# Moving all stores of a rotary-embedding kernel to SyncE's queue, in smaller pieces

## The chip, the cores and the metric

The kernel runs on one core of a Trainium2 chip. Times are microseconds (us) on the device; a kernel's time is the median of its runs. The "span" in a profile is shorter by about 1.8 us (84.47 us and 82.69 in the profiled run of the kernel before).

## The reference

```python
angles = np.outer(positions * scale, freqs)          # 1024 x 32
cos, sin = np.cos(angles), np.sin(angles)
x_first, x_second = x[..., :32], x[..., 32:]         # x: 8 x 8 x 1024 x 64, float32
out = concatenate([x_first * cos - x_second * sin,
                   x_first * sin + x_second * cos], axis=-1)
```

16.78 MB come in and 16.78 MB go out, with two multiplications and an addition per number. It is a problem of moving data.

## The kernel before

The 64 heads are cut into four units of 16 heads, 4.19 MB each. In memory a unit is 128 rows (one for each partition) of 32 KB. GpSimd loads the units and turns them into 2-byte numbers on the way (a casting load). VectorE rotates each unit in two halves, ScalarE casts each half back to 4 bytes in the tile `OUT`, and a DMA stores it. The half of the first unit that is needed last comes in by two plain loads instead, from SyncE and ScalarE.

```python
pin(nc.gpsimd.dma_start(out=Xf[0][:, :NH], in_=xv[0][:, :NH]))
...
for u in range(1, NU):
    c = C2 if u == NU - 1 else 0                       # C2 = 1024 columns
    pin(nc.gpsimd.dma_start(out=Xf[u][:, : N - c], in_=xv[u][:, : N - c]))
    if c:
        pin(nc.gpsimd.dma_start(out=Xf[u][:, N - c :], in_=xv[u][:, N - c :]))
...                                                    # tables of sine and cosine
for u in range(NU):
    OUT = xout.tile([P, N], FP32, tag="O")             # three buffers
    for s in range(2):
        ...                                            # four VectorE instructions
        pin(nc.scalar.copy(out=OUT[:, ns], in_=Xf[u][:, ns]))
        if u >= NU // 2:
            pin(nc.sync.dma_start(out=ov[u][:, ns], in_=OUT[:, ns]))
    if u < NU // 2:
        c = C1 if u == 0 else 0                        # C1 = 512 columns
        if c:
            pin(nc.gpsimd.dma_start(out=ov[u][:, :c], in_=OUT[:, :c]))
        pin(nc.gpsimd.dma_start(out=ov[u][:, c:], in_=OUT[:, c:]))
```

So the first two units are stored from GpSimd, behind the loads on the same queue, and the last two in halves from SyncE.

## Time and profile before

| | before |
|---|---|
| time, median of 6 runs (range) | 84.56 us (84.37 to 84.61) |
| span of the profiled run | 82.69 us |
| GpSimd's queue (q0): moved as it lands, share of 16 DMA engines | 15.73 MB, 66.7% |
| SyncE's queue (q1) | 9.44 MB, 27.3% |
| ScalarE's queue (q10) | 1.06 MB, 3.2% |
| VectorE, ScalarE busy | 60.3 us, 40.1 us |

The prediction takes the GB/s of a stretch to count packets at their landing, and puts the first packet at 1.3 us and the end of the last at 81.1 us. The packet records of the trace show that the views count a packet at its start. On the span's clock the first packet starts at 1.74 us and the last ends at 81.45 us. Every time of a packet below is on the span's clock.

### The profile page before, as it was taken

How to read it: one execution, taken by the hardware profiler on the slowest of the kernel's cores; microseconds unless marked ns; L12 is line 12 of the kernel's file. 1: busy time of each engine (PE TensorE's matmuls, PEld its weight loads, DVE VectorE, ACT ScalarE, POOL GpSimd, SP SyncE). 2: the span in 40 equal slices, each digit the busy share in tenths (PEclk: the TensorE clock that was granted, in tenths of full speed). 3: DMA queues.
4: the chain of work that ended last, by engine and by line, in shares of the span. 5: the costliest groups of instructions: out<-in, count | busy, mean ns of one | idle time of the engine just before them, and what ended most of it. 6: DMA issues, size and time to landing. Idle time of an engine off the chain costs nothing.

```text
span 82.7 us, 184 instructions
## 1 busy us (share of the span) xinstructions
PE 6.4 (8%) x18; PEld 2.4 (3%) x18; DVE 60.3 (73%) x40; ACT 40.1 (49%) x18; POOL 5.7 (7%) x16
## 2 busy tenths in 40 slices
PE   0011798200000000000000000000000000000000
PEld 0011232000000000000000000000000000000000
DVE  0306276999999999999999999999999997000000
ACT  0602159999960691294089049309705912950000
POOL 4950000000020002000000200000000000000000
PEclk9999999995555555555555555555555555555555
DMA  3899998996998999999499889989899899999991
GB/s 55 323 323 269 297 325 186 254 254 135 246 254 182 198 254 222 222 222 222 36 456 446 357 386 476 507 357 460 380 523 404 365 428 428 460 404 436 428 428 79
DMA packets 2099, 26.22 MB, mean 317 GB/s; under 512 B 371, under 2 KB 371, under 8 KB 563
## 3 DMA queue, kind: packets, MB, share of 16 engines
q0 software_dynamic: 1088, 15.73, 66.7%
q1 hardware_dynamic: 720, 9.44, 27.3%
q10 hardware_dynamic: 290, 1.06, 3.2%
q14 instruction: 1, 0.00, 0.0%
HBM read 16.79 MB, written 16.78 MB: 406 GB/s over the span
## 4 chain that ended last, share of the span: by engine, by line
DVE 54%; ACT 14%; issue 7%; DMA 6%; PE 5%; DVEq 1%; ACTq 0%
DVE X L158 19%; DVE pr L157 19%; DVE X L162 9%; DMA freq_row<-in_freqs_dram 6%; ACT T L144 5%; DVE X L159 5%; ACT OUT L165 4%; PE ps L134 4%; ACT X L145 4%; DVEq L203 1%; PE cfreq L102 1%; ACT tab L127 1%; DVE r L118 1%; DVE y L109 1%; ACTq L71 0%
## 5 line engine op out<-in xcount | busy, mean ns | idle before, releaser
L165 ACT CAST OUT<-X 128x4096 f32<-128x4096 f16 x8 | 28.8, 3605 | 24.2 <-DVE X L162 24.2
L157 DVE TENSOR_TENSOR pr<-X,T 128x4096 f16<-128x4096 f16 x8 | 18.3, 2292 | 1.0 <-ACT T L144 0.7
L158 DVE TENSOR_TENSOR X<-X,T 128x4096 f16<-128x4096 f16 x8 | 18.3, 2292 | 0.3
L159 DVE TENSOR_TENSOR X<-X,pr 128x2048 f16<-128x2048 f16 x8 | 9.8, 1225 | 0.3
L162 DVE TENSOR_TENSOR X<-pr,X 128x2048 f16<-128x2048 f16 x8 | 9.7, 1218 | 0.0
L144 ACT CAST T<-ps 128x1024 f16<-128x1024 f32 x6 | 5.7, 1030 | 2.6 <-PE ps L134 2.6
L134 PE MATMUL ps<-tab,sel 128*128 128x512 f16 x16 | 5.8, 503 | 2.6 <-ACT tab L127 2.2
L142 DVE CAST T<-ps 128x1024 f16<-128x1024 f32 x2 | 2.4, 1224 | 2.2 <-PE ps L134 2.2
L145 ACT CAST X<-X0f 128x4096 f16<-128x4096 f32 x1 | 3.6, 3650 | 0.0
L100 DVE COPY sel<-one 128x2048 f16<-128x2048 f16 x1 | 0.7, 694 | 2.8 <-POOL one L89 2.8
L122 ACT ACTIVATE tab<-r 128x256 f16<-128x256 f32 x1 | 0.4, 416 | 4.4 <-DVE r L118 4.4
L172 POOL DMA_DIRECT2D out_dram<-OUT x2 | 1.1, 531 | 20.2 <-ACT OUT L165 20.2
L122 ACT ACT_TABLE_LOAD x1 | 1.3, 1283 | 2.1 <-issue 2.1
L134 PEld LDWEIGHTS <-sel 128*128 128x128 f16 x16 | 1.9, 122 | 6.1 <-issue 5.7
L95 POOL DMA_DIRECT2D X<-in_x_dram x3 | 2.0, 658 | 0.0
L171 POOL DMA_DIRECT2D out_dram<-OUT x1 | 0.6, 554 | 19.1 <-ACT OUT L165 19.1
L105 DVE CAST posf<-pos_i 128x8 f32<-128x8 int32 x1 | 0.2, 173 | 2.2 <-DMA pos_i<-in_positions_dram 2.2
L102 PE MATMUL cfreq<-freq_row,coef 1*128 1x32 f32 x2 | 0.6, 391 | 5.9 <-DMA freq_row<-in_freqs_dram 5.9
L109 DVE TENSOR_TENSOR y<-posf,cfreq 128x256 f32<-128x256 f32 x1 | 0.4, 420 | 0.7 <-PE cfreq L102 0.7
L85 POOL DMA_DIRECT2D X<-in_x_dram x1 | 0.7, 669 | 0.8 <-POOLq L189 0.8
L102 PEld LDWEIGHTS cfreq<-freq_row,coef 1*128 1x128 f32 x2 | 0.5, 308 | 5.9 <-issue 5.9
L97 POOL DMA_DIRECT2D X<-in_x_dram x1 | 0.6, 557 | 0.0
(12 smaller groups left out, 2.8 us busy)
## 6 DMA issues: line engine op xcount, KB each, us to landing
out_dram<-OUT SPq DMA_DIRECT2D x4, 2048.0 KB, 11.6
X<-in_x_dram POOLq DMA_DIRECT2D x2, 2048.0 KB, 24.2
out_dram<-OUT POOLq DMA_DIRECT2D x1, 4096.0 KB, 20.4
out_dram<-OUT POOLq DMA_DIRECT2D x1, 3840.0 KB, 21.1
X<-in_x_dram POOLq DMA_DIRECT2D x1, 1792.0 KB, 37.5
X0f<-in_x_dram SPq DMA_DIRECT2D x1, 1024.0 KB, 4.7
X<-in_x_dram POOLq DMA_DIRECT2D x1, 1024.0 KB, 11.5
X0f<-in_x_dram ACTq DMA_DIRECT2D x1, 1024.0 KB, 13.4
```

The source lines that it names most:

```text
L95: pin(nc.gpsimd.dma_start(out=Xf[u][:, : N - c], in_=xv[u][:, : N - c]))
L102: nc.tensor.matmul(out=cfreq, lhsT=coef, rhs=freq_row, start=True, stop=True)
L122: pin(nc.scalar.activation(out=tab[:, 0], in_=r, func=AF.Sin, bias=0.0, scale=-_TWO_PI_DN))
L134: nc.tensor.matmul(out=ps[:, i].rearrange("p t w -> p (t w)"), lhsT=sel[:, g + i].rearrange("s h q -> s (h q)"), rhs=tab.rearrange("s t k ...
L142: pin(nc.vector.tensor_copy(out=dst, in_=ps))
L144: pin(nc.scalar.copy(out=dst, in_=ps))
L145: pin(nc.scalar.copy(out=Xf[0][:, NH:], in_=X0f[:, :NH]))
L157: pin(nc.vector.tensor_tensor(out=pr, in0=Xs, in1=sin_b, op=ALU.mult))
L158: pin(nc.vector.tensor_tensor(out=Xs, in0=Xs, in1=cos_b, op=ALU.mult))
L159: pin(nc.vector.tensor_tensor(out=Xs[:, :, 0, :], in0=Xs[:, :, 0, :], in1=pr[:, :, 1, :], op=ALU.subtract))
L162: pin(nc.vector.tensor_tensor(out=Xs[:, :, 1, :], in0=pr[:, :, 0, :], in1=Xs[:, :, 1, :], op=ALU.add))
L165: pin(nc.scalar.copy(out=OUT[:, ns], in_=Xf[u][:, ns]))
```

## The change

All stores go to SyncE. The first and the last unit leave in four DMAs each, of 8 KB rows; the two between in halves, of 16 KB rows. GpSimd is left with the loads. The intent is plain from the page: the first unit's stores wait some 18 us behind loads on GpSimd's queue (issued at 24.32 us, first row at 42.21), and on a queue of their own they could start at once.

```diff
-            if u >= NU // 2:
-                pin(nc.sync.dma_start(out=ov[u][:, ns], in_=OUT[:, ns]))
-        if u < NU // 2:
-            c = C1 if u == 0 else 0
-            if c:
-                pin(nc.gpsimd.dma_start(out=ov[u][:, :c], in_=OUT[:, :c]))
-            pin(nc.gpsimd.dma_start(out=ov[u][:, c:], in_=OUT[:, c:]))
+            parts = 2 if u in (0, NU - 1) else 1
+            for i in range(parts):
+                c = slice(s * NH + i * NH // parts, s * NH + (i + 1) * NH // parts)
+                pin(nc.sync.dma_start(out=ov[u][:, c], in_=OUT[:, c]))
```

More of the change, by code (lines that the diff above doesn't have):

```diff
@@ L47 @@
     W = K8 * half
-    C1 = 512
     C2 = 1024
```

## The prediction

> **What bounds the kernel now.** I read first the sixteen DMA engines' row over the span, then the queues with their bytes, then the table by stage, the waits of SyncE's queue, and last the chain of waits. The page has them so:
>
> ```profile
> span 82.7 us, 184 instructions
> PE 6.4 (8%) x18; PEld 2.4 (3%) x18; DVE 60.3 (73%) x40; ACT 40.1 (49%) x18; POOL 5.7 (7%) x16
> ...
> DMA  3899998996998999999499889989899899999991
> ...
> q0 software_dynamic: 1088, 15.73, 66.7%
> q1 hardware_dynamic: 720, 9.44, 27.3%
> q10 hardware_dynamic: 290, 1.06, 3.2%
> ...
> HBM read 16.79 MB, written 16.78 MB: 406 GB/s over the span
> ...
> DVE 54%; ACT 14%; issue 7%; DMA 6%; PE 5%; DVEq 1%; ACTq 0%
> ```
>
> The chain names VectorE (54%), and that misleads: it follows instructions back from the last one on an engine, and the last transfers are not in it. The three queues' packets took 66.7 + 27.3 + 3.2 = 97.2% of sixteen engines' span, so the DMA engines have something in hand from the first packet to the last. Q0 is GpSimd's queue. Its 15.73 MB are counted as they land: 8.39 MB of stores plus loads written as 2-byte numbers, which is half of what they read. So a load stretch shows about half the GB/s of a store stretch at the same pace, and has to be doubled before the two are compared:
>
> ```profile
> 1.30:4.00 2.70, 0.00 (x0) 0.00 (x0) 0.69 (x1) 1.28 (x1) 2.62 (x7) 1.00 0.84 269
> 24.00:36.00 12.00, 0.00 (x0) 0.00 (x0) 11.83 (x8) 5.00 (x3) 1.08 (x2) 0.50 1.02 218
> 38.50:42.50 4.00, 0.00 (x0) 0.00 (x0) 3.93 (x4) 0.82 (x1) 0.00 (x0) 0.50 0.91 139
> 44.00:56.00 12.00, 0.00 (x0) 0.00 (x0) 11.82 (x8) 5.12 (x3) 0.53 (x1) 0.50 1.03 444
> 68.00:80.00 12.00, 0.00 (x0) 0.00 (x0) 1.83 (x2) 3.60 (x1) 0.00 (x0) 0.50 1.00 430
> 81.10:82.70 1.60, 0.00 (x0) 0.00 (x0) 0.00 (x0) 0.00 (x0) 0.00 (x0) 0.50 0.00 0
> ```
>
> The columns are stretch, length, busy time of five engines, granted clock, DMA share and GB/s. Casting loads read 2 x 218 = 436 GB/s (24 to 36 us); stores from GpSimd go at 444 (44 to 56, where packets counted at their landing flatter it a little) and from SyncE at 430 (68 to 80). All three are one ceiling, near 432 GB/s or 27.0 bytes per ns and engine. Of the 33.57 MB moved, 33.57 / 432 = 77.7 us are pure transfer. The rest of 82.7 is 1.3 us before the first packet, 1.6 us after the last (receipt and closing), and about 2 us lost inside: the slow start (269 GB/s at 1.3 to 4), and one dip, at 38.5 to 42.5, where 139 GB/s land against 218. That is 4 x (1 - 139/218) = 1.5 us at most; packets in flight at its edges count against it, and I put the true loss at 1 us. The engines are "busy" all through it, so it is a stall of packets and not an empty queue. It falls where the 7168-column load of the last unit ends and its 1024-column remainder begins.
>
> The last proof is the end:
>
> ```profile
> 66.49 7.34 SPq L167 DMA_DIRECT2D out_dram<-OUT  x2
> ...
> 69.86 3.60 ACT L165 CAST OUT<-X 128x4096 f32<-128x4096 f16 x1 [3.40 <-DVE X L162]
> ```
>
> ScalarE ends at 73.46 and the last store of 2.10 MB is issued at once. Alone it would take 2.10 / 0.430 = 4.9 us, to 78.4. The last packet ends at 81.1: a backlog of 81.1 - 73.5 - 4.9 = 2.7 us of older stores lies ahead of it. So the arithmetic could be up to 2.7 us later, and a store could be issued earlier, without moving the end. Only bytes per ns, stalls, or an empty queue move it.
>
> **What the Trainium skill says.** "DMA: Bandwidth & Descriptors", section "Issuing engines are not separate DMA queues": DMAs from any issuing engine run on the same sixteen engines and interleave, and changing the issuer saves only sequencer time. The trace agrees: 444 and 430 GB/s for the two issuers. The same page, "Where 436 GB/s comes from", puts the ceiling at 435 GB/s for sixteen ports; the 430 to 444 here are that. The same page, "Queues, rings and completion order": each engine takes turns between queues, a packet at a time. The packet records of the trace show rows as packets: 1227 ns for a 32 KB load row, 611 ns for a 16 KB and 309 ns for an 8 KB row on q1. So after the change a load and a store queue share time by row size. "SBUF — State Buffer", "Who interferes with whom", says VectorE can starve GpSimd of the port with which it writes descriptors, and that SyncE's DMAs are immune. The trace shows nothing to win there: GpSimd's three store issues took 0.53 to 0.55 us each beside a busy VectorE, behind a queue that was full anyway.
>
> **The change part by part.** The streams of VectorE, ScalarE and TensorE are the same, instruction by instruction; GpSimd loses three issues, SyncE goes from four stores to eight. SyncE's last eight transfers gain waits on a reused completion counter; each refers to one eight transfers back, which for the last unit are the first unit's stores. By the simulation below they end by 52, against issues at 66 and 73: no cost.
>
> *Packets.* First unit: before, one piece of 0.26 MB (64 packets of 159 ns) and one of 3.93 MB (128 of 1138 ns), together 155.9 us of engine time, or 9.74 us over sixteen. After, 512 rows of 309 ns: 9.89. Second: before 128 x 1213 / 16 = 9.70, after 256 x 611 / 16 = 9.78. Third: same. Fourth: before 256 x 611 / 16 = 9.78, after 9.89. Sum +0.34 us.
>
> *Turn-taking.* The start has an example: 8 KB rows of q10 beside casting loads took 322 ns, 13 more than on q1. If every row that runs beside loads pays 13 ns: the first unit's rows then, some 300 to 500, cost 0.25 to 0.4 us.
>
> *Order.* Today the first unit's store, issued at 24.3, waits behind all loads and starts near 42. Now it starts near 26 and takes turns with them. Stepping through it packet by packet with the durations above: the third unit's load ends near 32.7 (was 31.5), the fourth's near 44 and 48 (was 41 and 42). VectorE wants them at 41.7 and 55.8 and 62.8. Margins of 9, 12 and 15 us, so no compute moves. The buffer that the fourth unit's cast reuses at 62.9 is free by about 54. The queue never empties, and the last packet comes at the same place plus the sums above.
>
> *The dip.* Up to 1.0 us could come back, if it belongs to all engines passing from long to short load packets at once, which interleaving smears. Nothing in the trace says so; I give it one half: -0.5.
>
> Total: +0.34 + 0.3 - 0.5 = +0.1 us, or nothing. The finer last pieces (8 KB rows) may even out sixteen engines' ends by 0.1 to 0.2 us. I predict 84.4.
>
> **Rivals.** First, *earlier stores shorten the tail*: the intent, I suppose. For it: stores wait 20 us today. Against it: those 20 us are a full DMA row; advancing bytes in a saturated queue only delays others, by conservation. It could give at most the 2.7 us of backlog, then the last store's own time binds: 73.5 + about 0.7 to its first packet + 4.9 + 1.6 = 80.7 us of span, time 82.5. Reaching that needs 2 us of lost time to vanish; I see 1.
>
> Second, *reads and writes mixed run at another pace*. The kernel before never mixes HBM reads with stores for long, so the trace is silent. If the 24 us of mixed stretch (26 to 50) ran 3% slower, 0.7 us are lost: 85.2; if faster by as much, 83.7.
>
> Third, *late loads stop VectorE*. If turns were not by row but favoured stores strongly, the fourth unit would come late: 8.4 MB of stores are issued before 45.3, and all of them ahead of the last loads would put these at 42 + 17 (the first four half-stores, 4.9 each, less what fits anyway) = near 59. The first half of that unit would wait 3 us; with 2.7 us of backlog as cushion, 0.5 us appears at the end, plus some empty queue: up to 86. Unlikely.
>
> Fourth, *the tail goes hollow*: if SyncE's in-order issue waits on a counter, a later store starts late. Then the share falls below full in the last ten slices; up to 85.5.
>
> **Range and chances.** The known terms cancel within half a microsecond; the dip and mixed pace give about 0.7 each way. I say 84.4, 83.4 to 85.4. Two per cent is 1.7 us: below 82.8 is almost the floor worked out above, chance 0.05; above 86.2 needs the third or fourth rival, 0.03; the rest 0.92.
>
> **What would show it.** Right: DMA row full to the end; HBM rate over the span still near 406; VectorE's and ScalarE's starts unchanged, ScalarE ending at 73.5; packets on q1 about 16.78 + 1.05 MB; loads of the last unit landing near 44 and 48; no dip, or the same dip near 47. Wrong: VectorE waiting for X at the fourth unit; the mixed stretch at a total clearly off 432 GB/s when loads are doubled; a store stretch with 8 KB rows below 425; the span under 81.

## The result, and the profile after

The changed kernel takes 84.67 us (median of 6 runs, 84.52 to 84.79); the kernel before took 84.56 in the same rounds. The ratio is 1.0017, with a 95% interval from 1.0002 to 1.0031. Ratios here divide the mean time of one kernel's runs by that of the other's runs of the same rounds, so they are not quite the ratio of the medians. The change costs some 0.1 us and is "the same" by any practical measure. 84.4 was predicted, with 83.4 to 85.4 as the range.

The page of the changed kernel, in the lines that answer to those of before:

```profile
span 83.0 us, 195 instructions
...
DMA  2899996998998988999796999999999999899991
...
q1 hardware_dynamic: 1872, 17.83, 51.4%
q0 software_dynamic: 720, 7.34, 42.8%
q10 hardware_dynamic: 290, 1.06, 3.2%
HBM read 16.79 MB, written 16.78 MB: 404 GB/s over the span
...
X<-in_x_dram POOLq DMA_DIRECT2D x1, 1792.0 KB, 41.3
...
X<-in_x_dram POOLq DMA_DIRECT2D x1, 256.0 KB, 44.6
```

8.39 MB have moved from q0 to q1. The sum of the shares is 97.4% where it was 97.2%, and the DMA row is as full as it was. The last two loads, issued at 4.1 and 4.6 us, now land 41.3 and 44.6 us later where they took 37.5 and 38.3: they share the engines with stores. Nothing waited for them. VectorE and ScalarE run the same sequence without a new wait, only some 0.35 us earlier, which they gained in the first 20 us. Where the last half begins (62.47) no wait is marked, and the last cast waits for VectorE alone:

```profile
60.08 1.23 DVE L158 TENSOR_TENSOR X<-X,pr 128x2048 f16<-128x2048 f16 x1
61.22 1.22 DVE L161 TENSOR_TENSOR X<-pr,X 128x2048 f16<-128x2048 f16 x1
62.47 2.29 DVE L156 TENSOR_TENSOR pr<-X,T 128x4096 f16<-128x4096 f16 x1
...
69.52 3.60 ACT L164 CAST OUT<-X 128x4096 f32<-128x4096 f16 x1 [3.40 <-DVE X L161]
```

The last cast starts at 69.52 us (69.86 before), and still the end is later. The table by stage has the same columns as before:

```profile
1.30:4.00 2.70, 0.00 (x0) 0.00 (x0) 0.69 (x1) 1.28 (x1) 2.62 (x7) 1.00 0.85 281
24.00:36.00 12.00, 0.00 (x0) 0.00 (x0) 11.83 (x8) 5.32 (x2) 0.00 (x0) 0.50 1.02 235
...
44.00:56.00 12.00, 0.00 (x0) 0.00 (x0) 11.83 (x8) 5.12 (x3) 0.00 (x0) 0.50 1.02 400
...
68.00:80.00 12.00, 0.00 (x0) 0.00 (x0) 1.48 (x2) 3.60 (x1) 0.00 (x0) 0.50 1.00 425
```

From 24 to 36 us 235 GB/s stand where there were 218, and from 44 to 56 us 400 for 444: stores are now spread among the loads, and loads count half, so neither figure says that anything is faster or slower. Only the stretch from 68 to 80 us compares directly, stores against stores: 425 GB/s with mostly 8 KB rows, 430 with 16 KB rows. That is just at the 425 below which the prediction wanted to be called wrong; it is not a sharp sign, as two kernels below with 16 KB rows throughout show ("changed, all 16 KB" has 425, "all 16 KB, last counter" 434).

What did move is the dip. The next two lines are GB/s from 24 to 32 us in slices of 0.2 us, first of the kernel before, then of the changed one. Sixteen DMA engines work in step, so each group of three or four numbers is one row on each engine, and the distance between groups is the time of one row.

```profile
GB/s 0 328 901 82 0 0 0 328 901 82 0 0 0 328 901 82 0 0 0 328 901 82 0 0 0 328 901 82 0 0 0 246 901 164 0 0 0 72 645 430
```

```profile
GB/s 0 492 655 164 0 0 0 492 655 164 0 0 0 0 410 819 82 0 0 0 0 0 287 369 860 369 82 0 0 41 287 532 860 164 82 0 0 82 287 573
```

Before, a load row of 32 KB takes six slices, 1.2 us, every time. In the changed kernel the distance grows to seven slices and then to about nine before the first store rows appear (the 287 and 369 in front of the 860 are where they mix in). The packet records give 1227 ns as the usual row, up to 1511 ns for rows that start near 25.5 us and up to 1694 ns near 27. SyncE had issued its first store at 23.70; its first row starts at 28.46. So most of the slow rows come while a store is already issued and has not yet begun; some more follow between 30 and 33 us.

To size such stalls I count the bytes that each stretch moved, with casting loads at the 4 bytes they read, and compare with 27.1 bytes per ns and engine (433 GB/s), the pace of undisturbed stretches. "Lost" below is the difference as time, worked out from the packet records of each run:

| lost, us | 24-36 | 36-46 | 46-56 | 56-66 | 66-80 | last packet ends | closing after it |
|---|---|---|---|---|---|---|---|
| before | 0.01 | 1.05 | 0.01 | 0.02 | 0.07 | 81.45 | 1.24 |
| changed | 0.89 | 0.13 | 0.17 | 0.05 | 0.15 | 81.78 | 1.23 |

One loss of 1.05 us has become one of 0.89, and small ones are added: mixing in the middle, 8 KB rows at the end (0.15 for 0.07). The sum of the five stretches rises by 0.23 us, from 1.17 to 1.40 before rounding of the parts. The profiled run of the changed kernel (84.79) is the slowest of its six, so these 0.2 us are rather more than the typical difference.

### The profile page after: what moved, and what is told of

The parts are those of the page before. It is cut to its first block, busy times and chain, and to the rows that moved or that the text cites. A ratio compares the mean times of both kernels' runs of the same rounds, so it can differ in the third digit from the quotient of the medians. Undisturbed runs are those within 1.5% of the kernel's fastest.

```text
span 83.0 us, 195 instructions
## 1 busy us (share of the span) xinstructions
PE 6.1 (7%) x18; PEld 2.4 (3%) x18; DVE 60.3 (73%) x40; ACT 40.1 (48%) x18; POOL 4.1 (5%) x13
## 3 DMA queue, kind: packets, MB, share of 16 engines
q10 hardware_dynamic: 290, 1.06, 3.2%
## 4 chain that ended last, share of the span: by engine, by line
DVE 54%; ACT 15%; issue 7%; DMA 5%; PE 5%; DVEq 1%; ACTq 0%
DVE X L157 19%; DVE pr L156 19%; DVE X L161 9%; ACT T L143 6%; DMA freq_row<-in_freqs_dram 5%; DVE X L158 5%; ACT OUT L164 4%; ACT X L144 4%; PE ps L133 4%; DVEq L197 1%; PE cfreq L101 1%; ACT tab L126 1%; DVE r L117 1%; DVE y L108 1%; ACTq L70 0%
## 5 line engine op out<-in xcount | busy, mean ns | idle before, releaser
L126 ACT ACTIVATE tab<-ra,quarter 128x256 f16<-128x256 f32 x1 | 0.5, 508 | 0.0
## 6 DMA issues: line engine op xcount, KB each, us to landing
X<-in_x_dram POOLq DMA_DIRECT2D x1, 1792.0 KB, 41.3
X<-in_x_dram POOLq DMA_DIRECT2D x1, 256.0 KB, 44.6
```

## The experiments

Twelve kernels were run; all gave correct results. The medians of the kernel before in their rounds were 84.47, 84.47 and 84.44.

My theory after the result was that the loss of about 1 us belongs to the passing from loads to stores, whoever issues them and wherever it falls. The rival was that in the kernel before it belonged to the short load of 1024 columns, and in the changed kernel to something else, such as SyncE's queue starting or the number of rows.

**First group.** The first kernel is the kernel before with one load for the whole last unit:

```diff
-        c = C2 if u == NU - 1 else 0
+        c = 0
```

> The kernel before, with the last unit's load in one piece in place of 7168 + 1024 columns. Theory (the dip is the price of passing from loads to stores, whoever issues them): a dip of about 1 us stays between 38 and 42 us; only the short rows' own cost goes, 128 x (172 + 1076 - 1227) ns / 16 = 0.17 us, so 84.4. Rival (the dip is the short load's): the dip is gone and the time is near 83.5.

The other three are the changed kernel with 16 KB rows for the first unit, for the last, and for both:

```diff
-            parts = 2 if u in (0, NU - 1) else 1
+            parts = 2 if u == NU - 1 else 1      # first unit in halves
+            parts = 2 if u == 0 else 1           # or: last unit in halves
+            parts = 1                            # or: all in halves
```

> The changed kernel, with the first unit's stores in halves of 16 KB rows (last unit still in 8 KB rows). Theory: 256 rows of 611 ns for 512 of 309 save 0.11 us, and half as many turns of 13 ns save up to 0.2 us: 84.4. The dip of about 0.6 us when the stores arrive near 25 us stays, since it goes with the change of direction. Rival (the dip at 25 us comes of the number of rows): it halves, 84.1. Rival (8 KB rows protect the loads): loads are late, but with 10 us of margin this costs nothing.

> The changed kernel, with the last unit's stores in halves of 16 KB rows (first still in 8 KB rows). Theory: 8 KB rows went at 26.7 bytes per ns and engine over the last ten us against 26.95 for 16 KB rows, so 0.1 us is saved: 84.6. Rival (finer rows at the end even out the engines): 84.8.

> The changed kernel, with all stores in halves of 16 KB rows from SyncE. Theory: sum of the two parts, 84.3; what is left against the kernel before is then the move to SyncE itself, with the dip at 25 us in place of the one at 40 us. Rival (parts don't add up): outside 84.2 to 84.5.

| | time | ratio to before (95%) | lost 24-36 | lost 36-46 | last packet ends | closing |
|---|---|---|---|---|---|---|
| before, whole last load | 84.51 | 1.0001 (0.9988 to 1.0014) | 0.01 | 0.87 | 81.49 | 1.24 |
| changed, first unit 16 KB | 84.71 | 1.0026 (1.0010 to 1.0043) | 0.76 | 0.08 | 81.55 | 1.35 |
| changed, last unit 16 KB | 84.71 | 1.0028 (1.0014 to 1.0042) | 0.47 | 0.33 | 81.59 | 1.35 |
| changed, all 16 KB | 84.77 | 1.0036 (1.0020 to 1.0051) | 0.72 | 0.08 | 81.50 | 1.47 |

The first row kills the rival for most of the loss in the kernel before. Its stages, with the last load in one piece:

```profile
36.00:38.50 2.50, 0.00 (x0) 0.00 (x0) 2.47 (x2) 1.90 (x1) 0.00 (x0) 0.50 0.98 210
38.50:42.50 4.00, 0.00 (x0) 0.00 (x0) 3.93 (x4) 1.16 (x1) 0.00 (x0) 0.50 0.90 161
...
44.00:56.00 12.00, 0.00 (x0) 0.00 (x0) 11.83 (x8) 5.12 (x3) 0.53 (x1) 0.50 1.00 431
```

It reads 161 GB/s at 38.5 to 42.5 us where the kernel before had 139, still far under 218. By the packet records, without a short load 0.87 us are lost at the same place; up to 0.18 of the 1.05 could be the short load's, though the kernel before with one more 128-byte load (third group), the same up to 52 us, lost 0.91 there. The time did not go to 83.5, nor did the 0.17 us of the short rows come back in the end; the sixteen engines finished 0.67 us apart in that run where it had been 0.38, and the last of them counts.

The other three rows went against my expectation. 16 KB rows should have saved 0.1 to 0.4 us, and the times did not fall at all. The traces show two opposite halves. The last packet does end earlier, by 0.19 to 0.28 us (81.50 to 81.59 for 81.78). But the closing after the last packet is longer, 1.35 and 1.47 us in place of 1.23, and that I had not counted. Nor did the turns become fewer. In the changed kernel 288 rows of 8 KB took 322 ns in place of 309; with all rows of 16 KB, 286 rows took 624 ns in place of 611. The 13 ns came about once for each load row beside the stores, whatever the store's row, and cost 0.23 us over sixteen engines in both.

These rows also show how far a stall varies. Up to its last unit, "last unit 16 KB" is the changed kernel, instruction by instruction, and yet it lost 0.47 and 0.33 us where the other lost 0.89 and 0.13.

**Second group.** Is the loss a price paid once, as for a path that is cold at the first store? Then a tiny early store would take it away. It went into both kernels:

```diff
+    wz = consts.tile([P, 128], FP32)
+    pin(nc.vector.memset(wz, 0.0))
+    pin(nc.sync.dma_start(out=ov[NU - 1][:, N - 128 :], in_=wz))
```

> The kernel before, with a 64 KB store of zeros from SyncE at the start (overwritten by the last store). Theory A (the first store after loads only is a cold path, warmed once): the dip of 1 us near 40 us is gone and the time is near 83.6. Theory B (each passing from loads to stores costs it): dip as before, 84.5 to 84.6.

> The changed kernel with the same early store. A: the loss of 0.9 us between 24 and 34 us is gone, 83.8 to 83.9. B: it stays, 84.7.

And what of a store is it that stalls the loads? Two kernels, made from the one before, put other transfers in the place where the changed kernel has its first stores. One adds plain loads, the other copies within on-chip memory:

```diff
             pin(nc.scalar.copy(out=OUT[:, ns], in_=Xf[u][:, ns]))
+            if u == 0:      # loads
+                pin(nc.sync.dma_start(out=X0f[:, s * 2048 : (s + 1) * 2048], in_=xv[0][:, s * 2048 : (s + 1) * 2048]))
+            if u == 0:      # or: copies
+                pin(nc.sync.dma_start(out=X0f[:, NH + s * 2048 : NH + (s + 1) * 2048], in_=OUT[:, ns.start : ns.start + 2048]))
```

> The kernel before, plus two plain loads of 1 MB in 8 KB rows from SyncE near 24 us into a dead buffer: 2.1 MB more, 4.9 us, so 89.4. If the loss at 25 us in the changed kernel comes of SyncE's queue starting beside casting loads, load rows are stretched here too (near 0.6 us lost between 24 and 30). If it comes of stores, there is none, and the 1 us dip comes when the loads end, near 44 to 47.

> The kernel before, plus two copies of 1 MB in 8 KB rows from on-chip memory to on-chip memory from SyncE near 24 and 31 us: 4.9 us more, 89.4. If reading on-chip memory amid loads is what stalls, near 0.6 us is lost at 24 to 34 and the dip at the end of the loads is smaller; if writing to HBM is, nothing is lost there and the dip at the end of the loads is whole.

| | time | lost 24-36 | lost 36-46 | lost 46-56 | last packet ends | closing |
|---|---|---|---|---|---|---|
| before + early store | 85.56 | 0.02 | 0.68 | 0.01 | 82.63 | 1.65 |
| changed + early store | 85.66 | 0.29 | 0.39 | 0.18 | 81.93 | 1.67 |
| before + loads on SyncE | 89.42 | 0.11 | 0.26 | 0.36 | 86.03 | 1.61 |
| before + on-chip copies | 89.73 | 0.49 | 0.43 | 0.08 | 86.33 | 1.61 |

The early store did not pay. The ratios are 1.0124 (1.0094 to 1.0154) and 1.0143 (1.0130 to 1.0156), and 0.7 us are still lost after it in both kernels. That is less than the 1.06 and 1.03 without it (24 to 46 us), but other kernels without an early store also show 0.7 to 0.9, so I don't call it an effect. Theory A falls. About 0.4 us of the extra time are again closing, and 0.3 more lie outside the span (2.07 us between time and span in both, where it was 1.78). In the first of them one DMA engine also ended 1.66 us after the earliest, in a run that was the slowest of six that spread from 85.11 to 86.34; why was not followed up.

The last two tell the parts of a store apart. GB/s from 24 to 32 us, with the extra loads and then with the copies:

```profile
GB/s 0 82 614 532 492 82 0 0 123 246 737 451 410 0 0 0 246 451 451 737 82 0 0 123 123 737 492 410 82 0 0 205 287 614 532 328 0 0 0 246
```

```profile
GB/s 0 246 655 410 0 0 0 246 655 410 0 0 0 246 655 410 0 0 0 82 328 369 410 573 0 0 41 123 492 410 492 410 0 0 123 164 369 410 737 164
```

With loads on SyncE's queue the new rows simply mix in: 0.11 us are lost in twelve, and between 24 and 34 us no load row takes over 60 ns more than usual. In the seven kernels whose 8 or 16 KB store rows begin there, 20 to 51 load rows do, and with the copies 36. So a second queue that starts beside casting loads is not enough to slow them, and writing to HBM is not needed, since the copies read and write on-chip memory. *Reading* on-chip memory is what the copies and the stores share and the extra loads lack.

That this is the cause is not shown, for three reasons. Each of the two is one look, and the size varies as said above. The extra loads were issued at 20.3 us, both at once, and not at 24 and 31. And "issuer only" (third group) speaks against it in this form: there the 2 KB store rows of the first 512 columns, which read on-chip memory too, ran beside the loads from 28.0 us on without one slow load row up to 35 us (0.08 us lost from 24 to 34). Its loss, 0.71 us from 34 to 39, came around the first 30 KB rows, which were issued at 31.2 and began at 38.25. So the stall belongs to long or many rows at least, and its cause stays open.

The 0.43 us that the copies show between 36 and 46 us lie in the last rows of the 7168-column load, where all sixteen engines have one slow row (between 42 and 44 us). "Changed + early store" and "changed, last unit 16 KB" lost 0.39 and 0.33 in that stretch without any copies, so this part is not put to their account. With the extra loads the loss at the end of the loads is 0.26 + 0.36 = 0.62 us, just before GpSimd's stores begin at 46.8.

**Third group: the closing.** In the trace, SyncE's last records are a row of waits on completion counters. Transfers issued by SyncE and ScalarE use eight counters in turn, and at the end SyncE checks them in order. The kernel before makes 8 such transfers and the changed one 16, so in both the last store is on the eighth counter and everything else has been checked by then. The three kernels with 16 KB rows make 14, 14 and 12: counter six, six and four. The kernels of the second group end on the first or the second. The theory is that each counter checked after the last store's costs 0.06 us. To test it, four loads of 128 bytes bring "all 16 KB" to 16 transfers, and one such load brings the kernel before to 9:

```diff
+            if u == 1 and s == 1:
+                for i in range(4):
+                    pin(nc.sync.dma_start(out=pad[:, i * half : (i + 1) * half], in_=freqs[None, :]))
```

> All stores in 16 KB halves from SyncE (as in the third form tried), plus four loads of 128 bytes on SyncE's queue, so that the last store falls on the last of the eight completion counters that SyncE checks at the end, as in the kernel before and in the changed one. Theory C (closing time after the last packet is 1.66 us plus 0.06 us for each counter checked after the last store's): 1.66 us again, last packet near 81.1, span near 82.75, time 84.5 to 84.55. Rival (closing time varies for another reason): 84.7 to 84.8 as without the loads.

> The kernel before, plus one load of 128 bytes on SyncE's queue amid the last four stores, so that the last store falls on the first counter. Theory C: closing 2.1 us in place of 1.66, time 84.9. Rival: unchanged, 84.5.

Two more go with them. In one the issuer alone changes; it keeps the store shapes of the kernel before, with five such loads:

```diff
-            pin(nc.gpsimd.dma_start(out=ov[u][:, c:], in_=OUT[:, c:]))
+            pin(nc.sync.dma_start(out=ov[u][:, c:], in_=OUT[:, c:]))    # and the same for the first 512 columns
```

> The kernel before with its store shapes kept (512 + 7680 columns, 8192 columns, then halves), all issued by SyncE, with five loads of 128 bytes so that the last store is on the last counter. It is the issuer alone. Theory: one loss of about 0.9 us moves from 38-42 us to 24-34 us, rows of 30 and 32 KB keep 27.0 bytes per ns and engine, last packet near 81.0 and closing 1.66: 84.5, the same as before. Rival (moving to SyncE costs of itself): 84.7.

The last joins what had looked useful: all stores in 16 KB halves from SyncE, the last counter, and the whole last load.

> As the first of this group, with the last unit's load in one piece as well. Theory: short rows saved, 0.17 us: 84.35 to 84.4, a little under the kernel before. Rival (nothing at this level adds up, since the slowest of sixteen engines ends it): 84.5.

| | time | ratio to before (95%) | last packet ends | closing |
|---|---|---|---|---|
| all 16 KB, last counter | 84.49 | 1.0005 (0.9992 to 1.0017) | 81.48 | 1.24 |
| before, first counter | 85.05 | 1.0069 (1.0056 to 1.0081) | 81.53 | 1.64 |
| issuer only, last counter | 84.59 | 1.0016 (1.0002 to 1.0030) | 81.52 | 1.30 |
| all 16 KB, last counter, whole load | 84.26 | 0.9987 (0.9975 to 1.0000) | 81.25 | 1.23 |

The end of the DMA row shows how little time lies between the last packets. The GB/s from 80 to 84 us, in slices of 0.1 us, of the kernel before, then of the changed one, then of the kernel before with one 128-byte load:

```profile
GB/s 164 1147 328 0 492 492 164 983 492 0 0 0 0 0 0 0 0 0 0 0 0 0 0 0 0 0 0 0 0 0 0 0 0 0 0 0 0 0 0 0
```

```profile
GB/s 573 328 410 492 410 410 492 410 410 410 492 246 492 164 82 0 0 0 0 0 0 0 0 0 0 0 0 0 0 0 0 0 0 0 0 0 0 0 0 0
```

```profile
GB/s 819 492 0 492 328 492 819 328 164 164 0 0 0 0 0 0 0 0 0 0 0 0 0 0 0 0 0 0 0 0 0 0 0 0 0 0 0 0 0 0
```

A packet stands in the slice where it starts, so 0.61 us have to be added for a 16 KB row and 0.31 for an 8 KB row. The last rows start between 80.8 and 80.9, 81.4 and 81.5, and 80.9 and 81.0 us, and end near 81.45, 81.78 and 81.53. The third kernel's data end 0.1 us after those of the first, and its span is 0.5 us longer.

The waits of SyncE's queue show where that is. These are the lines of the end: of the kernel before, of the changed one, and of the kernel before with one 128-byte load. The columns are the total wait, the number of waits and the longest.

```profile
SPq L203 <- DMA out_dram<-OUT: 7.5, 2, 4.8
```

```profile
SPq L197 <- DMA out_dram<-OUT: 7.4, 4, 2.4
```

```profile
SPq L207 <- DMA out_dram<-OUT: 8.0, 1, 8.0
```

In the first two SyncE goes through its counters as the last stores land, waits at two or four of them, and the longest wait is not the whole. In the third it stands at the very first counter for 8.0 us, until the last store has landed, and only then walks through the rest. Over all kernels: 1.23 to 1.24 us of closing with the last store on the eighth counter (1.30 once), 1.35 on the sixth, 1.47 on the fourth, 1.61 on the second, 1.64 to 1.67 on the first. The slope is (1.65 - 1.24) / 7 = 0.06 us a counter, as expected, and the trace shows the steps: in the third kernel the wait at the first counter is over at 81.86 us, and the seven checks after it start at 81.92, 81.99, 82.05, 82.11, 82.17, 82.23 and 82.29. One transfer of 128 bytes made the kernel before 0.6 us slower in time, 0.4 of it in closing.

With the counter put right, "all 16 KB" falls from 1.0036 to 1.0005, and the two intervals don't touch. The issuer alone comes to 1.0016 with losses of 0.15 and 0.68 us at 24-36 and 36-46. Moving stores to SyncE did not pay; by the interval it cost 0.02 to 0.3%, with five small loads and 0.06 us of closing in it.

The joined kernel is the fastest, 84.26 against 84.44. Its interval ends at 1.0000, so it is at best 0.1 to 0.2% better, and I don't claim that it beats the kernel before.

## Why the prediction was right

- **The bound.** Right. The DMA row is full to the end in both kernels, the shares are 97.2 and 97.4%, and the waits that the change shortened (18 us from issue to first row for the first store, 4.8 after) were worth nothing. What the prediction cites of the Trainium skill, "DMA: Bandwidth & Descriptors", "Issuing engines are not separate DMA queues", holds to within 0.3%: the issuer alone gave a ratio of 1.0016 (1.0002 to 1.0030). A store that goes earlier in a full queue pushes loads later: the last loads land at 45.4 and 49.2 us by their issues (4.1 + 41.3 and 4.6 + 44.6), a little over the predicted 44 and 48. VectorE, which wanted them at 55.4 and 62.5, did not notice. The first and the third rival, an earlier end and late loads, are both out, and so is the fourth: the last ten slices of the DMA row are as full as before.
- **Packets, +0.34 us.** In the trace the direction and about the size are there. In the last unit 0.08 us more were lost (0.15 for 0.07), where 0.11 had been added for its rows. Taking 8 KB rows out of both units moved the last packet by 0.28 us, where 2 x (9.89 - 9.78) = 0.22 had been worked out; but the engines' ends are 0.3 to 0.7 us apart in most of these runs, which is as much. In time, the changed kernel (1.0017) and "all 16 KB" on the same counter (1.0005) have intervals that overlap, so a cost of 8 KB rows in the time is not shown.
- **Turn-taking, +0.3 us.** Right in kind and near the low end in size: 288 rows paid the 13 ns, 0.23 us, where 300 to 500 rows and 0.25 to 0.4 us were expected. In the table by stretches, 0.30 us were lost between 36 and 56 us (0.13 + 0.17). 208 of these rows, 0.17 us, are in it; the joined kernel, without the short load, has 112 there and lost 0.12. What the rest of the 0.30 is was not separated. The second rival, another pace when reads and writes mix, is this 1 to 2% and no more, apart from the stall.
- **The dip, -0.5 us.** This is the step that failed. It is one term of the sum; the bound stands without it. The prediction gave one half to its going away, "if it belongs to all engines passing from long to short load packets at once", and if it stayed, it was to be near 47 us. It did neither. At 46 to 56 us only 0.17 us are lost; the loss of 1.05 us turned up as 0.89 us at 24-36 us, mostly before the first store rows, and it stays in the kernel before without the short load (0.87). Counted by the load rows alone (those over 60 ns longer than usual, by their excess over sixteen engines) it went from 0.95 to 0.83 us. The term should have been near -0.1; what the stall comes of stays open.
- **The end.** The 0.1 to 0.2 us for finer last rows did not come. The engines ended 0.51 us apart where it was 0.38.
- **Counters.** "No cost" was right, but not for the reason given. The prediction looked at the waits before stores only. That the last store stays on the last counter, from 8 transfers to 16, is luck; two transfers fewer and the closing would have grown by 0.1 us. The prediction also miscounts: SyncE goes from four stores to twelve, not eight (the page after has x8 and x4). Its eight waits and what they refer to are right all the same.
- **Order.** The first store row was put near 26 us and came at 28.46, and the last cast ended at 73.12, not 73.5. Nothing hung on either.

Without the dip's -0.5 the sum would have been +0.34 + 0.3 = +0.64 us. The trace shows +0.23 and the times +0.1. So the wrong credit for the dip covered two costs that were too large as a sum, and that the total came so near is luck. A likely reason, argued and not tested, is that they overlap: the first unit's 8 KB rows were charged once for their length and once more for their turns, and what was lost in the mixed stretch contains both. What carried the prediction is the mechanism, a full queue that no order can hurry; its small terms were right only as a sum.

## What to carry to other kernels

Where the DMA engines are full from start to end, the order of transfers and the engine that issues them were not levers here (1.0017 and 1.0016): count bytes, row sizes and stalls, and see whether anything waits for what comes later. When a dip in the DMA row seems to belong to one transfer, take that transfer away before crediting its return, and look at a second run of the same code, since a stall here varied by 0.4 us from one stretch to another. And when comparing kernels by tenths of a microsecond, check what follows the last packet: here the number of transfers, modulo eight, was worth up to 0.4 us of span and hid a gain.

## What the Trainium skill lacked or had wrong

- "DMA: Bandwidth & Descriptors", "Where 436 GB/s comes from", gives 435 GB/s for the sixteen ports, but says that between HBM and on-chip memory the HBM side binds, at about 358. Here it did not: undisturbed stretches ran at 27.1 bytes per ns and engine, 433 GB/s, for casting loads (by what they read) and for stores of 30 KB rows alike, on one core alone.
- The same page, "Latency and other measured facts", gives about 600 ns to the first byte for a DMA from SyncE. At the start of the span that agrees if the issue itself is left out: the issue ran from 0.74 to 1.12 us, and the first row began at 1.74, 0.62 us later. Beside 32 KB load rows it was 4.8 us from the start of the issue (23.70 to 28.46). The page has no figure for the first byte when the DMA engines are busy.
- No page has the stall of load rows around the time when long store rows begin: 0.66 to 1.06 us between 24 and 46 us in the kernels without extra transfers, and 0.49 us at 24 to 36 us with on-chip copies.
- No page has it that a store row beside loads takes 13 ns more, about once per load row, for 8 KB and 16 KB rows alike (322 for 309 ns, 624 for 611).
- No page has the cost of the closing checks: 0.06 us for each completion counter that is checked after the one of the last store.
